# An expert stage in two passes: all first products with the selection work spread between them, activations through DRAM, then all second products

## The chip, the cores and the metric

The kernel runs on one core of one Trainium2 chip. The metric is the device time of one launch in microseconds. Three runs are shown as the time before, and one further execution was profiled.

## The reference

A decoder trunk of two layers on 256 tokens of width 1024. Each layer has a mixer (a linear recurrence beside sparse attention; the change does not touch it), a layer norm, and then the expert stage below, followed by a second layer norm. Inputs, weights and result are float32.

```python
def _peer(x, wq, subkeys, u_tab, v_tab):          # T=256, D=1024, 8 heads, 128 keys, top 16
    q = (xf @ wq).reshape(T, PEER_HEADS, 2, PEER_KEY_DIM)
    s = jnp.einsum('thcd,ckd->thck', q, subkeys)
    sv, si = lax.top_k(s, PEER_TOPK)
    cand = (sv[:, :, 0, :, None] + sv[:, :, 1, None, :]).reshape(T, PEER_HEADS, PEER_TOPK * PEER_TOPK)
    cv, ci = lax.top_k(cand, PEER_TOPK)
    ea = jnp.take_along_axis(si[:, :, 0], ci // PEER_TOPK, axis=-1)
    eb = jnp.take_along_axis(si[:, :, 1], ci % PEER_TOPK, axis=-1)
    experts = (ea * PEER_KEYS + eb).reshape(T, PEER_HEADS * PEER_TOPK)      # of 16384
    gate = jax.nn.softmax(cv, axis=-1).reshape(T, PEER_HEADS * PEER_TOPK)
    act = jax.nn.gelu(jnp.einsum('cd,ced->ce', xf, u_tab[experts]))
    return jnp.einsum('ce,ced->cd', act * gate, v_tab[experts])
```

## The kernel before

The kernel computes the expert stage densely: for all 16384 experts, not only the chosen ones. The experts lie in 128 tiles of 128. For tile `a`, the first product (`u_tile`) multiplies the 512 KB table tile `u_tab[a]` with the transposed tokens and gives 128 experts x 256 tokens; two tiles share a PSUM bank, and after the odd one a gelu writes both, a pair, into a buffer `act` (256 KB). A matrix `G` (two halves of 64 tiles, in SBUF) holds the gate of every expert and token, zero for those not chosen. `w_pair` multiplies a pair by its part of `G`. The second product (`v_tile`) multiplies the result with the 512 KB tile `v_tab[a]` and adds it up in four PSUM banks over all 128 tiles.

Most products are made in three: an operand is split into a high part (`hi`, ScalarE, L104) and the remainder (`lo`, VectorE, or GpSimd for the first 14 tiles, L105), and hi x hi, lo x hi and hi x lo are added up (`col_mm`, L113; `v_mm`, L972). `w_split` (L963, L964) splits an activation in the same way. `raw_mm` (L140) is one plain float32 product that needs no split; it is used for the first products of tiles 14 to 33.

`G` needs the selection first: scores per head (`query`, `top`), two rounds of the best 16 on VectorE (`best16`, `pairs`), the index work of `L847` to `L888`, a transpose of the chosen indices and gates to `eT` and `gT`, and then 32 times `onehots`: two VectorE instructions build one-hot matrices for 8 tokens, TensorE multiplies them, ScalarE copies the product into `G`.

The order before: queries and top-k with 14 first products behind them; index work with first products of tiles 14 to 21; one-hots with those of tiles 22 to 33. Until `G` is there an activation pair can't be used, so these 17 pairs go to DRAM (`kept`, issued by ScalarE, L755). Then the dense loop runs over a sequence `seq` in which the 17 kept pairs are mixed with the 47 fresh ones: it fetches kept pairs (`fetch`, L954) two places ahead, makes first products of fresh pairs two places ahead, and makes the second products of the pair in turn. The last 8 tiles of layer 0 and 6 of layer 1 (`NTBS`) are left for the end, where they are mixed with the layer norm. During the last 16 turns the free parts of `G` take the layer norm's rows, the next layer's first weights and some last `v_tab` tiles (`pre`).

The buffers that set how far one engine may run ahead: `raw` 4 (table tiles as loaded), `hi` and `lo` 3 each, the split activations 4, `act` 8 pairs. A buffer is used again when all readers of its old content are done, and the buffers of one name are given out in the order of the program.

The order of instructions on each engine is fixed when the program is built, by a planner: it takes, in the order of the program, what is ready by its own estimates of durations. On the chip each engine then works through its list in that order.

Of the kernel before, what the change touches and what calls it, by code (L numbers as in the profile page):

```python
# [11 lines left out]
F32 = mybir.dt.float32  # L12
# [36 lines left out]
NACT = 8  # L49
NU0 = 11  # L50
NSP = 17
# [27 lines left out]
def trunk_kernel(ctx: ExitStack, tc: tile.TileContext, x, xt, cst, lam, pvec, brow, w_in, w_lx, w_v, w_q4, lru_w,  # L79
# [187 lines left out]
    for l in range(NL):  # L267
# [12 lines left out]

# [449 lines left out]
        with tc.tile_pool(name="peer", bufs=1, reuse_waits="tile") as pp:  # L730
# [5 lines left out]

# [22 lines left out]
            def u_pair(a0):  # L759
                u_tile(a0)  # L760
                u_tile(a0 + 1)

            with tc.tile_pool(name="topk", bufs=1, reuse_waits="tile") as tk:
                skt = tk.tile([128, 2, 128], F32, name="skt")
                nc.sync.dma_start(skt, sk[l])
                sv = tk.tile([128, 2, 8, 2, 16], F32, name="sv")
# [3 lines left out]
                cd = tk.tile([128, 2, 8, NCAND], F32, name="cd")  # L770
                c2 = tk.tile([128, 2, 8, NCAND], F32, name="c2")
                qhs = {}

                def query(h):
# [4 lines left out]
                    else:  # L779
                        ps = bank()  # L780
                        for c in range(2):
# [3 lines left out]
                            else:  # L785
                                col_mm(ps[:, c * 256:c * 256 + 256], wtile(wq[l, k], (8, 128), POOL), xT)
# [10 lines left out]
                def top(h):  # L797
                    qh = qhs.pop(h)
# [8 lines left out]
                    for tb in range(2):  # L807
                        for c in range(2):
                            k = tb * 2 + c
                            best16(sv[:, tb, h, c], si[:, tb, h, c], ss[:, k], s2[:, k])  # L810

                def pairs(h0, h1):

                    n = h1 - h0
                    a, b, o = sv[:, :, h0:h1, 0], sv[:, :, h0:h1, 1], cd[:, :, h0:h1]
                    for i in range(8):
                        DVE.tensor_tensor(o[:, :, :, OFF[i]:OFF[i] + CNT[i]],
                                          a[:, :, :, i:i + 1].to_broadcast([128, 2, n, CNT[i]]),
                                          b[:, :, :, :CNT[i]], op=ALU.add)
                    DVE.tensor_tensor(o[:, :, :, OFF[8]:NCAND], a[:, :, :, 8:16],  # L820
                                      b[:, :, :, 0:1].to_broadcast([128, 2, n, 8]), op=ALU.add)
                    for h in range(h0, h1):
                        for tb in range(2):
                            best16(cv[:, tb, h], ci[:, tb, h], cd[:, tb, h], c2[:, tb, h])

                query(2)
                q_rows(1)
                query(0)
                top(2)
                query(1)  # L830
                top(0)
                query(3)
                top(1)
                for h in range(4, 8):
                    query(h)
                    top(h - 1)
                    if h == 5:
                        pairs(0, 4)
                top(7)
                for a in range(NPOOL):  # L840
                    u_tile(a)
                pairs(4, 8)

                gt = tk.tile([128, 16, 16], F32, name="gt")
# [428 lines left out]
```

## Time and profile before

| | us |
|---|---|
| three runs: median (lowest, highest) | 1966.04 (1962.35, 1966.09) |
| the profiled execution, its own time | 1961.14 |
| span of its trace | 1959.4 |
| TensorE busy in the span | 1913.2 |
| VectorE, ScalarE, GpSimd busy | 1285.2, 920.1, 126.0 |

The span goes from the first to the last instruction. Busy time counts an engine's instructions; TensorE's matmuls overlap and their ends are modelled, so two starts tell more than one duration. SPq and ACTq are DMA issues of SyncE and ScalarE; a row's time there is that of the issue and not of the transfer. In square brackets stands the idle time before an instruction, and what ended it.

### The profile page before, as it was taken

The numbers are of one execution on the slowest core, as the hardware profiler recorded it, in microseconds if no ns is written. First come the engines' busy times: TensorE is split into PE (matmuls) and PEld (weight loads), VectorE is DVE, ScalarE is ACT, GpSimd is POOL, SyncE is SP. The second block draws the span as 40 slices with busy tenths as digits, with TensorE's granted clock in tenths as the row PEclk, the third lists the DMA queues.
The fourth block names the chain that finished last, engine by engine and source line by source line (L and its number), as shares of the span: only waits on it lengthen the run. The fifth ranks groups of instructions, "written<-read, shape, count | busy, mean of one in ns | idle before, by whom it ended". The sixth has DMA issues, their size and how long they took to land.

```text
span 1959.4 us, 31424 instructions
## 1 busy us (share of the span) xinstructions
PE 1913.2 (98%) x12260; PEld 1676.5 (86%) x12260; DVE 1285.2 (66%) x2477; ACT 920.1 (47%) x1533; POOL 126.0 (6%) x71
## 2 busy tenths in 40 slices
PE   8999899999999999999999998999999999999998
PEld 7758898888888899999877488889888888999997
DVE  5756989565656555565567579896655665556555
ACT  3634425545454444454445344255545445445442
POOL 0005600000000000000000056000000000000000
PEclk9999899999999999999999999999999999999999
DMA  7405453666666666676362055436666676656552
GB/s 279 158 1 157 155 152 110 207 208 197 205 200 220 213 208 210 211 250 191 97 225 66 1 165 159 153 109 220 197 200 200 209 219 213 198 184 221 186 187 93
DMA packets 103017, 344.55 MB, mean 176 GB/s; under 512 B 12626, under 2 KB 13396, under 8 KB 102740
## 3 DMA queue, kind: packets, MB, share of 16 engines
q1 hardware_dynamic: 97972, 333.63, 53.6%
q10 hardware_dynamic: 4896, 8.92, 1.2%
q8 instruction: 96, 1.57, 0.3%
q14 instruction: 53, 0.43, 0.1%
HBM read 332.54 MB, written 9.96 MB: 175 GB/s over the span
## 4 chain that ended last, share of the span: by engine, by line
PE 87%; DVE 8%; DMA 2%; issue 2%; ACT 1%; POOL 1%; SPq 0%; DVEq 0%; POOLq 0%; ACTq 0%
PE ps L972 36%; PE ps L113 34%; PE ps L140 5%; PE ps L120 3%; PE ps L592 3%; DVE og L927 2%; DVE oh L923 2%; PE ps L934 2%; PE ps L564 1%; PE ps L517 1%; DMA raw<-in_wq_dram 1%; DVE si L795 1%; PE ps L233 1%; DVE s L793 1%; POOL lo L105 1%
## 5 line engine op out<-in xcount | busy, mean ns | idle before, releaser
L105 DVE TENSOR_TENSOR lo<-raw,hi 128x1024 fp32r<-128x1024 f32 x460 | 562.6, 1224 | 426.7 <-ACT hi L104 426.6
L104 ACT CAST hi<-raw 128x1024 fp32r<-128x1024 f32 x508 | 532.5, 1050 | 551.3 <-PE ps L113 321.0
L113 PE MATMUL ps<-xThi,hi 128*128 128x256 f32 x2080 | 594.2, 286 | 10.5 <-ACT hi L104 10.5
L113 PE MATMUL ps<-xThi,lo 128*128 128x256 f32 x2080 | 591.3, 284 | 5.9 <-POOL lo L105 5.1
L113 PE MATMUL ps<-xTlo,hi 128*128 128x256 f32 x2080 | 590.8, 284 | 0.0
L972 PE MATMUL ps<-hi,W 128*128 128x512 f32 x1936 | 550.5, 391 | 1.6 <-ACT W L963 1.6
L113 PEld LDWEIGHTS ps<-xThi,hi 128*128 128x128 f32 x2080 | 401.1, 193 | 18.8 <-ACT hi L104 10.9
L972 PEld LDWEIGHTS ps<-hi,W 128*128 128x128 f32 x1936 | 351.9, 189 | 65.8 <-ACT W L963 1.8
L113 PEld LDWEIGHTS ps<-xTlo,hi 128*128 128x128 f32 x2080 | 401.0, 193 | 7.3
L113 PEld LDWEIGHTS ps<-xThi,lo 128*128 128x128 f32 x2080 | 400.7, 193 | 6.6 <-POOL lo L105 5.7
L972 PE MATMUL ps<-lo,W 128*128 128x512 f32 x968 | 299.4, 390 | 0.0
L972 PEld LDWEIGHTS ps<-lo,W 128*128 128x128 f32 x968 | 181.8, 188 | 39.8
L963 ACT CAST W<-act 128x256 fp32r<-128x256 f32 x242 | 92.3, 405 | 145.9 <-PE ps L972 139.0
L140 PE MATMUL ps<-xTf,raw 128*128 128x256 f32 x704 | 158.1, 381 | 0.0
L140 PEld LDWEIGHTS ps<-xTf,raw 128*128 128x128 f32 x704 | 131.5, 190 | 17.6 <-issue 1.0
L105 POOL TENSOR_TENSOR lo<-raw,hi 128x1024 fp32r<-128x1024 f32 x48 | 122.5, 2566 | 329.6 <-ACT hi L104 329.5
L964 DVE TENSOR_TENSOR W<-act,W 128x256 fp32r<-128x256 f32 x242 | 97.3, 421 | 34.0 <-PE ps L972 31.5
L752 ACT ACTIVATE act<-ps 128x512 f32<-128x512 f32 x128 | 76.0, 593 | 92.8 <-PE ps L140 78.6
L950 DVE TENSOR_TENSOR act<-act,G 128x512 f32<-128x512 f32 x128 | 87.8, 686 | 44.5 <-DMA act<-kept 44.5
L938 ACT ACTIVATE G<-ps 128x256 f32<-128x256 f32 x256 | 74.8, 425 | 33.6 <-PE ps L934 31.9
L927 DVE TENSOR_TENSOR og<-oh,gT 128x2048 f16<-128x2048 f16 x64 | 76.0, 1219 | 0.7
L923 DVE TENSOR_TENSOR oh<-iota,eT 128x2048 f16<-128x2048 f16 x64 | 76.1, 1217 | 0.0
(256 smaller groups left out, 1293.0 us busy)
## 6 DMA issues: line engine op xcount, KB each, us to landing
raw<-in_u_tab_dram SPq DMA_DIRECT2D x256, 512.0 KB, 3.6
raw<-in_v_tab_dram SPq DMA_DIRECT2D x256, 512.0 KB, 3.6
raw<-in_w_in_dram SPq DMA_DIRECT2D x24, 512.0 KB, 4.5
raw<-in_wq_dram SPq DMA_DIRECT2D x24, 512.0 KB, 3.9
kept<-act ACTq DMA_DIRECT2D x34, 256.0 KB, 4.0
act<-kept SPq DMA_DIRECT2D x34, 256.0 KB, 4.3
ow<-in_w_out_dram SPq DMA_DIRECT2D x16, 512.0 KB, 7.4
qf<-in_w_q_dram SPq DMA_DIRECT2D x8, 512.0 KB, 3.8
```

Of the source, the lines that this page charges most:

```text
L104: ACT.copy(hi, raw)
L105: lo_eng.tensor_tensor(lo, raw, hi, op=ALU.subtract)
L113: PE.matmul(ps, a[m], b[n], start=start and i == 0, stop=stop and i == 2)
L140: PE.matmul(ps, raw[:, c], xTf[:, c], start=c == 0, stop=c == NCH - 1)
L752: ACT.activation(at.rearrange("p a b -> p (a b)"), ps, AF.Gelu_apprx_tanh)
L923: DVE.tensor_tensor(oh.rearrange("p q w a i -> p (q w) a i"), iota.unsqueeze(1).to_broadcast([128, 8, 128, 2]), eT[:, qs].rearrange("p q w ...
L927: DVE.tensor_tensor(og, oh[:, :, 0:1].to_broadcast([128, 4, 2, 128, 2]), gT[:, qs].unsqueeze(3).to_broadcast([128, 4, 2, 128, 2]), op=ALU. ...
L938: ACT.activation(G[g][:, :, t1:t1 + 4], ps.rearrange("p (t g a) -> p g a t", g=2, a=64)[:, g], AF.Copy, scale=1.0 / GSC)
L950: DVE.tensor_tensor(act[a0], act[a0], G[a0 // 64][:, a0 % 64:a0 % 64 + 2, :], op=ALU.mult)
L963: ACT.copy(whi, at[:, a % 2])
L964: DVE.tensor_tensor(wlo, at[:, a % 2], whi, op=ALU.subtract)
L972: PE.matmul(accs[tb * 2 + hf], ww[m][:, TB[tb]], v[n][:, hf * 512:hf * 512 + 512], start=a == first[0] and (m, n) == (0, 0), stop=a == 127 ...
```

## The change

All 128 first products come first. They are all split products (no `raw_mm` among them), and every activation pair goes to DRAM. The selection work is written as a generator that yields a cost after each piece; between pieces first products are issued so that the sum of costs is balanced, and it works in two halves of four heads. The queries of heads 4 to 7 are split on VectorE. The first products that are left are spread evenly between the 32 one-hot groups, which have buffers of their own. Then a second loop fetches pairs in order, two and three places ahead, and makes all second products. `act` has 4 buffers. Cut to its core:

```diff
-NACT = 8
-NU0 = 11
-NSP = 17
+NACT = 4
             def u_tile(a):
-                if NPOOL <= a < 2 * NSP:
-                    raw_mm(ps[:, HALF[a % 2]], rtile(u_tab[l, a], (8, 128)))
-                else:
-                    col_mm(ps[:, HALF[a % 2]], wtile(u_tab[l, a], (8, 128), POOL if a < NPOOL else DVE), xT)
+                col_mm(ps[:, HALF[a % 2]], wtile(u_tab[l, a], (8, 128), POOL if a < NPOOL else DVE), xT)
                 if a % 2:
                     at = act_tile()
                     ACT.activation(at.rearrange("p a b -> p (a b)"), ps, AF.Gelu_apprx_tanh)
-                    if a // 2 < NSP:
-                        kept[a - 1] = spill.tile([128, 2, S], F32, name="kept%d" % (a - 1), bufs=1)
-                        ACT.dma_start(kept[a - 1], at)
-                    else:
-                        act[a - 1] = at
+                    kept[a - 1] = spill.tile([128, 2, S], F32, name="kept%d" % (a - 1), bufs=1)
+                    ACT.dma_start(kept[a - 1], at)
...
-                                col_mm(ps[:, c * 256:c * 256 + 256], wtile(wq[l, k], (8, 128), POOL), xT)
+                                col_mm(ps[:, c * 256:c * 256 + 256], wtile(wq[l, k], (8, 128), POOL if h < 4 else DVE), xT)
...
+                def choices(g):
+                    DVE.tensor_tensor(gt, cv[:, g], cv[:, g, :, 0:1].to_broadcast([128, 8, 16]), op=ALU.subtract)
+                    ACT.activation(gt, gt, AF.Exp)
...
+                    yield 1.2
...
+                def work():
+                    for h in (2, 0, 1, 3):
+                        yield from top(h)
+                    yield from pairs(0)
+                    yield from choices(0)
+                    for h in range(4, 8):
+                        query(h)
+                        yield 2.44 - 5.76
+                        yield from top(h)
+                    yield from pairs(1)
+                    yield from choices(1)
+                    yield 0.0
+                    yield from turn_round()
...
+                for cost in work():
+                    room -= cost
+                    while room < 0 and a < 96:
+                        u_tile(a)
+                        room += 2.88 if a < NPOOL else 1.66
+                        a += 1
...
-                    oh = ring.tile([128, 4, 2, 128, 2], F16, tag="lo", name="oh")
-                    og = ring.tile([128, 4, 2, 128, 2], F16, tag="hi", name="og")
+                    ohg = (state.tile([128, 2, 4, 2, 128, 2], F16, tag="xTf", name="ohg") if t0 % 16 else
+                           pp.tile([128, 2, 4, 2, 128, 2], F16, name="ohg"))
+                    oh, og = ohg[:, 0], ohg[:, 1]
...
+                a0 = a
                 for i in range(32):
                     onehots(8 * i)
-                    while au < 2 * NSP and (au - 2 * NU0 + 1) * 32 <= (i + 1) * (2 * NSP - 2 * NU0):
-                        u_tile(au)
-                        au += 1
+                    while a < 128 and (a - a0) * 32 < (i + 1) * (128 - a0):
+                        u_tile(a)
+                        a += 1
...
+                seq = list(range(0, 128, 2))
...
                 for j, p in enumerate(body):
                     ready(j + 2)
-                    n = min(more_u(j + 2), len(todo)) if j < len(body) - 1 else len(todo)
-                    for _ in range(max(0, (n + 1) // 2)):
-                        u_tile(todo.pop(0))
+                    ready(j + 3)
                     v_tile(p)
-                    for _ in range(max(0, n - (n + 1) // 2)):
-                        u_tile(todo.pop(0))
                     w_pair(seq[j + 1])
                     v_tile(p + 1)
```

## Rows read from the trace of the kernel before

**Rows 1.** The page, parts 1 and 2: busy time of the engines, and the granted TensorE clock in 40 equal slices (tenths of full speed, 9 is 90% or more).

```profile
PE 1913.2 (98%) x12260; PEld 1676.5 (86%) x12260; DVE 1285.2 (66%) x2477; ACT 920.1 (47%) x1533; POOL 126.0 (6%) x71
PEclk9999899999999999999999999999999999999999
```

**Rows 2.** Busy time by stage: the stretch, its length, then PE, PEld, DVE, ACT and POOL busy (instructions), granted clock, DMA share, GB/s. The first three rows are layer 0 (top-k and index work; one-hots; dense loop), the last two the first two of these stages in layer 1.

```profile
150.00:272.00 122.00, 112.61 (x792) 106.05 (x791) 101.95 (x451) 43.25 (x58) 61.24 (x24) 0.96 0.52 163
272.00:352.00 80.00, 78.80 (x738) 71.27 (x737) 76.91 (x70) 43.39 (x138) 0.00 (x0) 1.00 0.41 122
352.00:935.00 583.00, 581.44 (x3570) 523.81 (x3569) 345.39 (x405) 288.22 (x379) 0.00 (x0) 1.00 0.66 210
...
1130.00:1250.00 120.00, 110.15 (x787) 104.75 (x787) 101.95 (x450) 43.17 (x57) 61.25 (x24) 0.97 0.53 166
1250.00:1326.00 76.00, 74.80 (x718) 67.73 (x717) 74.85 (x67) 40.29 (x132) 0.00 (x0) 1.00 0.40 116
```

**Rows 3.** The same columns in stretches of 10 us, two in the top-k stage of each layer.

```profile
220.00:230.00 10.00, 2.34 (x10) 1.90 (x9) 9.93 (x40) 5.11 (x6) 4.72 (x2) 0.66 0.13 35
230.00:240.00 10.00, 10.00 (x73) 10.00 (x72) 10.00 (x4) 3.29 (x4) 10.00 (x4) 0.83 0.60 194
1190.00:1200.00 10.00, 7.53 (x63) 7.33 (x62) 10.00 (x75) 1.97 (x3) 2.40 (x1) 1.00 0.55 163
1200.00:1210.00 10.00, 4.51 (x21) 4.22 (x22) 9.93 (x16) 5.11 (x6) 7.05 (x3) 0.66 0.26 78
```

**Rows 4.** The waits between 150 and 352 us: who waited for whom, us in total, times, the longest.

```profile
ACT gt L848 <- DVE gt L847: 9.2, 1, 9.2
...
PE ps L113 <- ACT hi L104: 5.1, 1, 5.1
...
PE ps L113 <- POOL lo L105: 2.5, 1, 2.5
```

**Rows 5.** Timeline of TensorE in the one-hot stage: start, time, engine, line, operation, count. One plain float32 first product is 16 entries, one one-hot group 16.

```profile
299.86 3.67 PE L140 MATMUL ps<-xTf,raw 128*128 128x256 f32 x16
303.36 2.00 PE L934 MATMUL ps<-og,oh 128*128 128x128 f16 x32
```

**Rows 6.** Timeline of TensorE in the dense loop: the first matmul of a first product and of the second product behind it; and the first of three second products in a row and of the first product behind them.

```profile
705.60 0.28 PE L113 MATMUL ps<-xThi,hi 128*128 128x256 f32 x1
...
708.48 0.63 PE L972 MATMUL ps<-hi,W 128*128 128x512 f32 x2
...
401.90 0.63 PE L972 MATMUL ps<-hi,W 128*128 128x512 f32 x2
...
410.08 0.28 PE L113 MATMUL ps<-xThi,hi 128*128 128x256 f32 x1
```

**Rows 7.** The page, part 5: groups of instructions, with busy time, mean ns of one, and the idle time before them.

```profile
L105 DVE TENSOR_TENSOR lo<-raw,hi 128x1024 fp32r<-128x1024 f32 x460 | 562.6, 1224 | 426.7 <-ACT hi L104 426.6
...
L964 DVE TENSOR_TENSOR W<-act,W 128x256 fp32r<-128x256 f32 x242 | 97.3, 421 | 34.0 <-PE ps L972 31.5
...
L950 DVE TENSOR_TENSOR act<-act,G 128x512 f32<-128x512 f32 x128 | 87.8, 686 | 44.5 <-DMA act<-kept 44.5
```

**Rows 8.** Timeline of VectorE in the dense loop of layer 0, in a stretch without products with G.

```profile
379.71 0.43 DVE L964 TENSOR_TENSOR W<-act,W 128x256 fp32r<-128x256 f32 x1 [0.48 <-PE ps L972]
380.73 1.23 DVE L105 TENSOR_TENSOR lo<-raw,hi 128x1024 fp32r<-128x1024 f32 x1 [0.59 <-ACT hi L104]
382.43 0.43 DVE L964 TENSOR_TENSOR W<-act,W 128x256 fp32r<-128x256 f32 x1 [0.48 <-PE ps L972]
```

**Rows 9.** Timeline of all engines around one fetch of layer 0, of which SyncE's, VectorE's and one of ScalarE's rows are shown. The first product with G is that of a fresh pair, the second that of the fetched one.

```profile
435.30 0.43 SPq L954 DMA_DIRECT2D act<-kept  x1
...
437.56 0.69 DVE L950 TENSOR_TENSOR act<-act,G 128x512 f32<-128x512 f32 x1
...
438.20 1.05 ACT L104 CAST hi<-raw 128x1024 fp32r<-128x1024 f32 x1 [1.32 <-PE ps L972]
...
439.05 0.69 DVE L950 TENSOR_TENSOR act<-act,G 128x512 f32<-128x512 f32 x1 [0.81 <-DMA act<-kept]
...
439.66 1.22 DVE L105 TENSOR_TENSOR lo<-raw,hi 128x1024 fp32r<-128x1024 f32 x1
...
440.80 0.42 DVE L964 TENSOR_TENSOR W<-act,W 128x256 fp32r<-128x256 f32 x1
```

**Rows 10.** The same around one fetch of layer 1.

```profile
1455.26 0.43 SPq L954 DMA_DIRECT2D act<-kept  x1
...
1460.96 0.69 DVE L950 TENSOR_TENSOR act<-act,G 128x512 f32<-128x512 f32 x1 [2.75 <-DMA act<-kept]
```

**Rows 11.** Timelines of SyncE and ScalarE at the start of the dense loop: two loads for second products, the gelu of the last kept pair, and the fetches of the first two pairs.

```profile
347.18 1.34 SPq L102 DMA_DIRECT2D raw<-in_v_tab_dram  x2
...
352.53 0.60 ACT L752 ACTIVATE act<-ps 128x512 f32<-128x512 f32 x1 [0.69 <-PE ps L140]
...
352.56 0.90 SPq L954 DMA_DIRECT2D act<-kept  x2
```

**Rows 12.** The page, part 6: the fetches (count, KB each, median us from issue to landing); and the view of tile `kept`, which takes writes and fetches together: who waited for it (us, times), and the times to landing.

```profile
act<-kept SPq DMA_DIRECT2D x34, 256.0 KB, 4.3
...
  DVE act L950: 44.5, 30
...
DMA to landing us min/median/max: 2.0/4.1/6.6
```

More of the change, by code (lines that the diff above doesn't have):

```diff
@@ L826, in trunk_kernel @@
[L826 to L844, printed above, removed]
@@ new lines, in top, with pairs @@
+                            best16(sv[:, h // 4, j, c], si[:, h // 4, j, c], ss[:, k], s2[:, k])
+                            yield 1.45
+                def pairs(g):
+                    a, b = sv[:, g, :, 0], sv[:, g, :, 1]
+                    for i in range(8):
+                        DVE.tensor_tensor(cd[:, :, OFF[i]:OFF[i] + CNT[i]], a[:, :, i:i + 1].to_broadcast([128, 8, CNT[i]]),
+                                          b[:, :, :CNT[i]], op=ALU.add)
+                        if i % 4 == 3:
+                            yield 1.2
+                    DVE.tensor_tensor(cd[:, :, OFF[8]:NCAND], a[:, :, 8:16],
+                                      b[:, :, 0:1].to_broadcast([128, 8, 8]), op=ALU.add)
+                    for j in range(8):
+                        best16(cv[:, g, j], ci[:, g, j], cd[:, j], c2[:, j])
+                        yield 1.05
@@ L903, in trunk_kernel @@
-                for a0 in range(2 * NU0 - 2, 2 * NU0, 2):
-                    u_pair(a0)
+                    yield 2.3
+                    DVE.tensor_tensor(t3, t3, sif[:, :, 1].unsqueeze(2).to_broadcast(shp), op=ALU.mult)
+                    yield 1.2
+                    tree(of(ev[:, 1], g), t3)
+                    DVE.tensor_reduce(gs, gt, axis=AX.X, op=ALU.add)
+                    DVE.reciprocal(gs, gs)
+                    DVE.tensor_tensor(of(gate, g), gt.rearrange("p (b h) k -> p b h k", b=2),
+                                      gs.rearrange("p (b h) -> p b h", b=2).unsqueeze(3).to_broadcast([128, 2, 4, 16]), op=ALU.mult)
@@ L906, in trunk_kernel @@
+                for h in (2, 0, 1, 3):
+                    if h == 0:
+                        q_rows(1)
+                    query(h)
+                a, room = 0, 0.0
+                for cost in work():
[4 more added lines that the diff above has]
+                        a += 1
             with tc.tile_pool(name="dense", bufs=1, reuse_waits="tile") as dp:
@@ L985, in v_tile @@
                         v_mm(a, ww, v, tb)
-                seq, k = [], 0
-                for i, f in enumerate(fresh):
-                    while k < NSP and k < 1 + (i + 1) * NSP / (0.55 * len(fresh)):
-                        seq.append(2 * k)
-                        k += 1
-                    seq.append(f)
+                seq = list(range(0, 128, 2))
                 tailp = list(range(nv, 128, 2))
@@ L1042, in trunk_kernel @@
                       [(pre_wv, i) for i in range(3) if more]
[L1043 to L1049 removed]
                 def ready(j):
[L1052 removed]
+                    if j < len(seq) and seq[j] not in act:
                         fetch(seq[j])
@@ L1056, in trunk_kernel @@
                     ready(j)
-                for _ in range(2):
-                    u_tile(todo.pop(0))
                 w_pair(body[0])
@@ L1081, in trunk_kernel @@
                             f(i)
-                assert not pre and not todo, (pre, todo)
+                assert not pre, pre
                 gb = ln_gb(new_gb, (l, 2))
+                for j in range(len(body), len(seq)):
+                    ready(j)
                 for p in tailp[1:]:
```

119 lines of the change are left out of this document (49 added, 70 removed).

## The prediction

> **What bounds the kernel now.** I read the page's shares first: TensorE is busy 98% of the span, VectorE 66%, ScalarE 47% [rows 1]. Busy matmul time overstates, so I read the stages next. From 352 to 935 us (interleaved first and second products of layer 0) TensorE does not pause: 581.4 of 583 us, while VectorE has work for 345 of them, and the DMA engines move 210 GB/s [rows 2]. TensorE sets the pace there and can be made faster only by less work. It loses time only before that: 9.4 us of idling in 150 to 272 us and 1.2 us in 272 to 352, and 9.9 and 1.2 us in the same stages of layer 1 [rows 2]. Within them stand the largest gap and a half clock: in 220 to 230 us TensorE worked 2.34 of 10 us at a granted clock of 0.66, and was at 0.83 in the ten after; in layer 1 4.51 us at 0.66 [rows 3]. The waits say why: ScalarE's exponential of the gates stood 9.2 us for VectorE, with the splits of the next table tiles queued behind it, and TensorE then waited 5.1 us for ScalarE and 2.5 us for GpSimd [rows 4].
>
> **First pass: what the change takes away.** (1) Of each layer's 34 spilled tiles 20 went through the plain float32 product. One takes 3.50 us (from 299.86 to 303.36, [rows 5]); the split product takes 2.88 us (705.60 to 708.48, [rows 6]). 40 tiles at 0.62 us: -25 us.
> (2) TensorE's idling in these stages sums to 21.7 us over both layers [rows 2], and the half clock costs another 4: 10 us at 0.83 lose 1.7, and 2.34 and 4.51 us at 0.66 lose 0.8 and 1.5 [rows 3]. So 26 us are to be had if top-k work is always covered by first products. VectorE can carry it on average: today's 102 us of top-k stage, 77 us of one-hots [rows 2] and 122 low parts (114 table tiles, 8 query tiles) at 1.22 us [rows 7] are 328 us, against 128 x 2.88 + 32 x 0.93 (half of 1.86 us for two one-hot groups, [rows 5]) + 8 x 2.88 = 421 us of TensorE. But in the top-k stretch itself the two are level by the diff's own costs, and the exponential that blocked ScalarE now comes twice per layer. Bounds: all of the 26 us, or none and as much lost again. I take half, -13 us. First pass: -38 us (from -51 to +1).
> (3) The 47 further spills per layer are issued from ScalarE at about 0.4 us each (a fetch's issue takes 0.43, [rows 9]), some 20 us; ScalarE is idle for half of the dense loop [rows 2] and nothing on the path waits for it, so nothing is added. Were ScalarE full it would be these 20 us per layer.
>
> **Second pass: what the change adds.** A second product takes TensorE 2.73 us (three from 401.90 to 410.08, [rows 6]), a pair 5.46. Per pair VectorE has two low parts (1.22), two split remainders (0.42) and one product with G (0.69), 3.97 us [rows 7]. Capacity is there. DMA would be 1.25 MB per pair at 5.46 us, 240 GB/s, beside 210 now [rows 2]; near, but not over.
>
> The price is in a ring. Only four activation buffers are left, and every pair is fetched. The fetch of pair j+3 needs the buffer of pair j-1, free when VectorE has made the remainder of that pair's second tile. Whatever pair number the loop fetches ahead, the ring closes after four. What matters is where the planner puts the product of the fetched pair in VectorE's order. It runs instructions as soon as it believes their inputs are there, not in program order: the first two fetches stand after two loads of second-product tiles that the program issues later, at the moment when the gelu before them in the ring got its buffer [rows 11]. And it believes that a fetch lands sooner than it does: the fetch at 435.30 has its product as the next thing on VectorE at 438.24, but the data let it start at 439.05; in layer 1 it is 1455.26 and 1460.96, a stall of 2.75 us [rows 9, 10]. 30 of 34 fetched pairs stalled VectorE, 44.5 us in all [rows 12]. Today that is hidden: eight buffers, no fetch waits for a recent VectorE instruction, and TensorE runs on from tiles split ahead.
>
> In a steady run of second products VectorE goes remainder 379.71, low part 380.73, remainder 382.43, and so on every 2.72 us, with gaps of about 0.5 us between [rows 8]. Put the changed kernel on this pattern: the remainder ending at 380.14 frees the buffer, the fetch goes at once, and a product put 2.94 us later falls at 383.1, into the gap ahead of the next low part and ahead of the remainder that frees the next buffer (about 385.15). As VectorE works in order, this gives a closed chain: remainder, fetch, landing, product, low part, remainder. Its length: 0.05 (semaphore) + 4.3 from issue to landing [rows 12] + 0.61 from product to low part + 1.14 from low part to remainder [rows 9] + 0.42 [rows 7] = 6.52 us per pair, against TensorE's 5.46. The loss is 1.06 us for each of 60 and 61 pairs in the two layers, 128 us; tiles split ahead cover about 4 us per layer, so +120 us. Bounds: with the quick landing (435.30 to 439.05, 3.75 us, [rows 9]) the chain is 5.97 us and the loss 54 us; with the slow one (5.70 us, [rows 10]) 7.92 us and 290 us. I take the median of the 34 fetches, since each pair adds its own latency and the load is about today's (1.25 MB in 6.5 us is 200 GB/s).
>
> By the Trainium skill, "DMA: Bandwidth & Descriptors", section "Anatomy of one DMA", a transfer costs about 2.0 us and its bytes at 436 GB/s, an estimate of 2.6 us for 256 KB. By that the chain would be 4.8 us and would not bind; the fetches of this trace, at a median of 4.3 us, do not agree.
>
> (4) At the end of the second pass the next layer's weights, last tiles and the layer norm's rows are loaded beside pairs that now take half the time of today's mixed ones; the eight extra high and low parts on VectorE and 16 norm instructions at about 0.7 us go into its waits in part. I add 4 us, from 0 to 10.
>
> **Sum.** -38 + 120 + 4 = +86 us. The profiled execution took 1961.1 us (its span 1959.4), so 2047 us. The median of the three runs shown, 1966.0, is 4.9 us above that execution; a measurement of this kernel tells about 0.2%, or 4 us, from no change.
>
> **Rivals.**
> A: the ring does not bind, since the product is put behind the freeing remainder. Place: VectorE's order, once per pair; it decides when the planner's latency is above some 5.0 us (385.15 less 380.14), or above 3.3 us with a low part in front, which shortens the chain to 5.4 us. For it: in today's rows I know only that the product came before the next low part, 4.0 us after the fetch at most [rows 9]. Against: it stands there each time the data are late. Then the second pass runs at TensorE's pace: -38 + 4, 1927 us (1910 to 1965). This is the case on the other side.
> B: landing is under 3.2 us, so that the chain is below 5.46 us. The quickest of all spill transfers took 2.0 us, the median 4.1 [rows 12], and 30 of 34 were late. Also 1927 us. It is what the rule of the page would give.
> C: the ring is slack and the first pass is worse: the exponential holds ScalarE twice per layer, nothing is recovered and as much is added, -25 + 26 + 5, 1967 us, no change. For it the 9.2 us [rows 4]; against it, tiles split ahead on VectorE and shorter halves.
> D: the product is put ahead of a whole remainder and two low parts: 4.3 + 0.05 + 0.61 + 0.33 + 1.14 + 1.14 + 0.42 = 7.99 us per pair, 2.53 x 121 = 306 us, less 8 and 34, 2225 us. Only if the planner's latency is much under 2 us.
> A half clock in the second pass I leave out: gaps of 2.5 us in ten (1190 to 1200) left it at 1.00 [rows 3].
>
> **Chances.** The forecast 0.60, A 0.23, B 0.05, C 0.07, D 0.05. The forecast's own range, from its bounds: quick landings and the whole first-pass gain, 54 - 51 + 0, give 1964; the median landing with a first pass at +1 and 10 at the end gives 2092; a little slower landings 2100. To hold eight in ten the range reaches into A and B: 1923 to 2100, which leaves out D, the upper end of the forecast and half of A's lower part. Slower: the forecast nearly whole, and D, 0.65. Faster: A and B nearly whole, 0.28. Same: C and the edges, 0.07.
>
> **What would show it.** Right: in the second pass VectorE idles about 3 us per pair before the product with G, released by the fetch; pairs come every 6 to 7 us; TensorE has gaps of about 1 us per pair, and SyncE's fetches follow VectorE's remainder. First pass: no plain float32 product, 2.88 us per tile, less than 13 us of gaps. Wrong: pairs every 5.46 us with TensorE solid (A, B), or gaps of TensorE in the first pass that exceed today's (C). What would upset the sum most is the planner's order on VectorE, which today's trace shows only for rings of eight.

## The result, and the profile after

| | before | after |
|---|---|---|
| median of four runs (lowest, highest), us | 1965.12 (1962.35, 1966.09) | 1986.91 (1984.31, 1991.17) |
| span of the profiled execution | 1959.4 | 1984.6 |
| first load of the selection, layer 0 and layer 1 | 148.9, 1126.1 | 151.1, 1146.7 |

The ratio is 1.0115 (95% interval 1.0094 to 1.0136): 22 us slower, where +82 us over the median had been forecast. By the loads in the last line, layer 0 takes 18.4 us longer, layer 1 4.6 us, and 2.2 us lie ahead of both.

Busy time by stage after, layer 0 (columns as in [rows 2]: stretch, length, PE, PEld, DVE, ACT, POOL, clock, DMA share, GB/s): top-k and index work, one-hots, the rest of the first pass, the boundary between the passes, and the second pass.

```profile
150.00:272.00 122.00, 114.29 (x871) 108.86 (x869) 81.53 (x315) 54.96 (x72) 39.24 (x16) 0.97 0.58 186
272.00:352.00 80.00, 74.00 (x595) 72.88 (x594) 66.44 (x196) 35.65 (x45) 0.00 (x0) 0.96 0.60 193
352.00:620.00 268.00, 268.00 (x2479) 266.67 (x2479) 169.68 (x141) 142.84 (x248) 0.00 (x0) 1.00 0.63 202
620.00:640.00 20.00, 15.12 (x61) 12.32 (x60) 12.45 (x19) 8.12 (x14) 0.00 (x0) 0.83 0.64 210
640.00:780.00 140.00, 140.00 (x620) 115.91 (x619) 95.86 (x129) 75.30 (x103) 0.00 (x0) 1.00 0.74 241
...
780.00:860.00 80.00, 73.39 (x310) 58.32 (x309) 52.14 (x73) 37.33 (x52) 0.00 (x0) 0.98 0.76 244
860.00:940.00 80.00, 76.91 (x328) 60.44 (x327) 51.88 (x69) 42.15 (x59) 0.00 (x0) 1.00 0.83 272
```

Two things are to be seen. The second pass is not slow from its start: 640 to 780 us has no gap. It loses time at its end, and more than the busy column says: at full pace 80 us hold 354 second-product matmuls (a row of the kernel with halved fetches, below), here they hold 310 and 328. That is 70 fewer at 80/354 = 0.226 us, some 16 us. And the first pass, which was to lose its gaps, has them at three places in each layer. Here they are in layer 0 in stretches of 5 us, with the waits that stand in them:

```profile
210.00:215.00 5.00, 1.73 (x13) 1.34 (x11) 4.93 (x32) 1.82 (x3) 0.50 (x1) 0.97 0.00 0
215.00:220.00 5.00, 2.25 (x11) 2.14 (x11) 5.00 (x5) 3.18 (x4) 2.80 (x1) 0.50 0.35 101
...
340.00:345.00 5.00, 1.06 (x10) 0.82 (x8) 4.97 (x6) 1.54 (x2) 0.00 (x0) 0.94 0.62 175
345.00:350.00 5.00, 4.85 (x31) 4.86 (x32) 3.67 (x4) 1.32 (x4) 0.00 (x0) 0.50 0.25 91
...
620.00:625.00 5.00, 1.16 (x10) 0.96 (x8) 1.87 (x3) 1.54 (x2) 0.00 (x0) 0.93 0.66 211
625.00:630.00 5.00, 3.95 (x9) 3.15 (x10) 3.19 (x7) 1.42 (x4) 0.00 (x0) 0.50 0.86 309
```

```profile
ACT gt L834 <- DVE gt L833: 7.4, 1, 7.4
...
PE ps L111 <- ACT hi L102: 3.3, 1, 3.3
...
PE ps L111 <- POOL lo L103: 2.7, 1, 2.7
...
PE ps L945 <- DVE ohg L938: 4.1, 1, 4.1
...
PE ps L983 <- ACT W L974: 4.9, 1, 4.9
```

The first place is the exponential's, as in [rows 4], with two waits of TensorE behind it (3.3 and 2.7 us). The second is new: TensorE has run all first products issued so far and waits for the first one-hots. The third, also new, is the boundary: the first fetches are issued behind table loads, and the second products wait for the first split activation. After each, TensorE ran at a granted clock of 0.50, the 1.2 GHz level, in the next five microseconds. The kernel before had one such place in layer 0, and by stretches of five microseconds its clock falls as low: TensorE was busy for 0.14 us of 220 to 225 us, and at 0.50 in 225 to 230 (the 0.66 of [rows 3] is a mean over ten).

The chain in the second pass, in VectorE's timeline and in SyncE's (fetches only), first in the stretch without gaps. A remainder (L975) is the rest of a split activation, a low part (L103) that of a table tile, and the landing is the time from a fetch's issue until VectorE has the data:

```profile
663.07 0.42 DVE L975 TENSOR_TENSOR W<-act,W 128x256 fp32r<-128x256 f32 x1
...
667.38 0.69 DVE L961 TENSOR_TENSOR act<-act,G 128x512 f32<-128x512 f32 x1 [0.97 <-DMA act<-kept]
667.99 0.42 DVE L975 TENSOR_TENSOR W<-act,W 128x256 fp32r<-128x256 f32 x1
...
672.41 0.69 DVE L961 TENSOR_TENSOR act<-act,G 128x512 f32<-128x512 f32 x1 [2.38 <-DMA act<-kept]
673.02 1.22 DVE L103 TENSOR_TENSOR lo<-raw,hi 128x1024 fp32r<-128x1024 f32 x1
674.16 0.42 DVE L975 TENSOR_TENSOR W<-act,W 128x256 fp32r<-128x256 f32 x1
```

```profile
663.56 0.42 SPq L965 DMA_DIRECT2D act<-kept  x1
...
668.44 0.33 SPq L965 DMA_DIRECT2D act<-kept  x1
...
674.65 0.42 SPq L965 DMA_DIRECT2D act<-kept  x1
```

Remainder, fetch, landing, product, remainder: the closed chain is there. But a low part stands between product and remainder only in every second pair (in 12 of 25 products of 645 to 780 us). In the two steps shown a fetch follows the one before it after 4.88 and 6.21 us; over the 25 products the mean distance is 5.46 us, TensorE's own pace. So here the chain costs nothing.

It does so at the end of layer 0's second pass. From 780 to 940 us a low part stands between in 18 of 26 pairs, nine times in a row around these lines (again VectorE, then the fetch between them on SyncE):

```profile
842.10 0.69 DVE L961 TENSOR_TENSOR act<-act,G 128x512 f32<-128x512 f32 x1 [1.87 <-DMA act<-kept]
842.71 1.22 DVE L103 TENSOR_TENSOR lo<-raw,hi 128x1024 fp32r<-128x1024 f32 x1
843.84 0.42 DVE L975 TENSOR_TENSOR W<-act,W 128x256 fp32r<-128x256 f32 x1
...
850.44 0.69 DVE L961 TENSOR_TENSOR act<-act,G 128x512 f32<-128x512 f32 x1 [4.71 <-DMA act<-kept]
```

```profile
844.33 0.42 SPq L965 DMA_DIRECT2D act<-kept  x1
```

The landings are longer there too (median 4.1 us and up to 6.0 in 780 to 860 us, against 3.8 and 4.4 before 780), and products come 6.23 us apart. The chain as it was forecast, with a landing of 4.1, gives 6.3. For 25 distances 0.77 us over TensorE's pace are 19 us, and tiles split ahead cover about 4: that is the 16 us counted above. In layer 1 (1780 to 1900 us) it is 10 of 21 pairs and 5.74 us, and less is lost.

The page sums VectorE's waits for the fetches, and shows the landing over the whole pass; against [rows 7, 12] four times the waiting at a shorter landing:

```profile
L961 DVE TENSOR_TENSOR act<-act,G 128x512 f32<-128x512 f32 x128 | 88.4, 692 | 172.9 <-DMA act<-kept 170.3
...
kept<-act ACTq DMA_DIRECT2D x128, 256.0 KB, 2.5
act<-kept SPq DMA_DIRECT2D x128, 256.0 KB, 3.8
```

### The profile page after: what moved, and what is told of

It is laid out like the page before. It is cut to its first block, busy times and chain, and to the rows that moved or that the text cites. A ratio compares the mean times of both kernels' runs of the same rounds, so it can differ in the third digit from the quotient of the medians.

```text
span 1984.6 us, 32589 instructions
## 1 busy us (share of the span) xinstructions
PE 1910.3 (96%) x12580; PEld 1681.0 (85%) x12580; DVE 1322.8 (67%) x2553; ACT 976.4 (49%) x1579; POOL 82.0 (4%) x55
## 4 chain that ended last, share of the span: by engine, by line
PE 80%; DMA 9%; DVE 6%; issue 2%; ACT 1%; POOL 0%; SPq 0%; POOLq 0%; DVEq 0%; ACTq 0%
PE ps L111 41%; PE ps L983 25%; DMA act<-kept 6%; PE ps L945 3%; PE ps L589 3%; PE ps L118 2%; DVE lo L103 2%; DMA raw<-in_v_tab_dram 1%; PE ps L231 1%; PE ps L797 1%; PE ps L561 1%; PE ps L514 1%; DVE W L975 1%; PE ps L369 0%; POOL lo L103 0%
## 5 line engine op out<-in xcount | busy, mean ns | idle before, releaser
L103 DVE TENSOR_TENSOR lo<-raw,hi 128x1024 fp32r<-128x1024 f32 x516 | 629.6, 1222 | 267.3 <-ACT hi L102 266.8
L111 PE MATMUL ps<-xThi,hi 128*128 128x256 f32 x2400 | 692.0, 288 | 6.5 <-ACT hi L102 6.5
L111 PE MATMUL ps<-xThi,lo 128*128 128x256 f32 x2400 | 683.5, 285 | 8.3 <-POOL lo L103 6.0
L111 PE MATMUL ps<-xTlo,hi 128*128 128x256 f32 x2400 | 682.8, 285 | 0.0
L111 PEld LDWEIGHTS ps<-xThi,lo 128*128 128x128 f32 x2400 | 463.6, 193 | 10.6 <-POOL lo L103 6.9
L111 PEld LDWEIGHTS ps<-xThi,hi 128*128 128x128 f32 x2400 | 464.1, 193 | 7.9 <-ACT hi L102 6.9
L111 PEld LDWEIGHTS ps<-xTlo,hi 128*128 128x128 f32 x2400 | 464.1, 193 | 0.3
L975 DVE TENSOR_TENSOR W<-act,W 128x256 fp32r<-128x256 f32 x242 | 101.0, 420 | 10.3 <-PE ps L983 8.1
L103 POOL TENSOR_TENSOR lo<-raw,hi 128x1024 fp32r<-128x1024 f32 x32 | 78.5, 2460 | 315.5 <-ACT hi L102 315.5
L938 DVE TENSOR_TENSOR ohg<-ohg,gT 128x2048 f16<-128x2048 f16 x64 | 78.2, 1225 | 2.1
L945 PE MATMUL ps<-ohg 128*128 128x128 f16 x1024 | 71.5, 222 | 8.2 <-DVE ohg L938 8.2
L934 DVE TENSOR_TENSOR ohg<-iota,eT 128x2048 f16<-128x2048 f16 x64 | 77.9, 1220 | 1.7 <-PE ps L945 1.7
```

Source lines behind the costliest of these rows:

```text
L103: lo_eng.tensor_tensor(lo, raw, hi, op=ALU.subtract)
L111: PE.matmul(ps, a[m], b[n], start=start and i == 0, stop=stop and i == 2)
L934: DVE.tensor_tensor(oh.rearrange("p q w a i -> p (q w) a i"), iota.unsqueeze(1).to_broadcast([128, 8, 128, 2]), eT[:, qs].rearrange("p q w ...
L938: DVE.tensor_tensor(og, oh[:, :, 0:1].to_broadcast([128, 4, 2, 128, 2]), gT[:, qs].unsqueeze(3).to_broadcast([128, 4, 2, 128, 2]), op=ALU. ...
L945: PE.matmul(ps[:, k * 128:k * 128 + 128], oh[:, q, 1, :, i], og[:, q, w, :, i], start=w == 0, stop=w == 1)
L975: DVE.tensor_tensor(wlo, at[:, a % 2], whi, op=ALU.subtract)
```

## Experiments on the first pass

All times are medians of at least four runs; the kernel before had 1964.0 to 1965.0 us beside them. Edits are to the changed kernel (1986.9 us).

**Plain products back for 20 tiles.**

```diff
+                if NPOOL <= a < 34:
+                    raw_mm(ps[:, HALF[a % 2]], rtile(u_tab[l, a], (8, 128)))
+                else:
                     col_mm(...)
```

> The first products of tiles 14 to 33 go through the plain float32 product again, as before the change, and so need no low part on VectorE. If TensorE sets the pace of the first pass, 40 tiles at 0.62 us add 25 us: 2012 us. Rival, VectorE's low parts are what makes the gaps of the top-k stretch (6 us and a half clock at 205 to 225, 4 us at 341): part of them goes, and the time is 1985 to 2000 us.

2005.7 us, ratio 1.0211 (1.0194 to 1.0228): +19 of the 25. The shorter products are a real gain of the change, most of it on the path.

**The exponentials late.** Both softmaxes move behind the index work.

```diff
                     yield from choices(1)
+                    softmax(0)
+                    softmax(1)
```

> The softmax of the first four heads' gates is made together with that of the last four, at the end of the selection work. Theory: the gap of TensorE at 210 to 217 us and its half clock after it (some 8 us per layer) come from ScalarE's exponential that stands 7.4 us for VectorE with two splits behind it; without it the time is 1971 to 1977 us. Rival: VectorE is late as such, and its low parts or another ScalarE instruction make the same gap: 1983 to 1990 us.

1991.9 us, 1.0145 (1.0127 to 1.0162): a miss, nothing gained. TensorE still waits there, 4.0 us in place of 6.0, mostly for GpSimd's low part (200 to 240 us):

```profile
PE ps L111 <- POOL lo L103: 2.9, 1, 2.9
PE ps L111 <- ACT hi L102: 1.1, 1, 1.1
```

**No exponential.** This kernel leaves out `ACT.activation(gt, gt, AF.Exp)`.

> Leaves out the exponential of the gates (they stay differences of scores, so the weights are not those of the reference). Theory: ScalarE's 7.4 us wait for VectorE ahead of the exponential delays the high parts behind it, from which TensorE's gap of 6.0 us and the half clock after it come in each layer: about 8 us per layer, -16 us, 1971 us. Rival: VectorE is the late one in that stretch and the low parts come too late whatever ScalarE does: within 5 us of the changed kernel.

1988.2 us, 1.0122 (1.0105 to 1.0138): the time is the rival's. With the exponential gone one wait of TensorE is left in 205 to 232 us, for VectorE, where there were two:

```profile
PE ps L111 <- DVE lo L103: 3.3, 1, 3.3
```

So ScalarE's 7.4 us explain less than half of the waiting there (2.7 of 6.0 us). TensorE got 2.7 us back in 200 to 240 us (36.65 us at 0.96, against 33.98 at 0.91), but the whole kernel did not get faster, and where the gain went is not shown. What is late besides is VectorE, full in that stretch (9.93 of 10 us in 210 to 220 us of the changed kernel).

**The last three pairs kept.** First products in the order 6 to 127, 0 to 5; the last three pairs stay in their buffers and are used first, so that the second pass starts without a fetch.

```diff
+                a = (n + 6) % 128
...
+                    if a < 6:
+                        act[a - 1] = at
+                        return
```

> First products are made in the order of tiles 6 to 127, 0 to 5, and the last three pairs made are not sent to DRAM but used first in the second pass. Theory: the gap of 4.9 us between the passes and the half clock after it (some 7 us per layer) come from the first fetch, which SyncE could issue only at 620.9 us; now only the last one-hot group is waited for: -8 to -14 us, 1973 to 1979 us. Rival: the gap is moved to the first fetched pair: 1984 to 1990 us.

1961.9 us, 0.9984 (0.9972 to 0.9996): -25, twice what was expected. The boundary of layer 0 (600 to 640 us) went from 35.12 us at 0.91 to full speed, which is 4.9 us of gap and 0.09 x 40 = 3.6 us of clock. In layer 1 it was 34.85 us at 0.96, 5.2 and 1.6 us: 15 us for both, where the expectation had some 7 for each and took from half to all of it. Another 5 us came from the end of layer 0's second pass, and some 4 from its 200 to 240 us (36.06 us at 0.96, against 33.98 at 0.91); neither had been expected.

```profile
600.00:640.00 40.00, 40.00 (x264) 36.08 (x263) 25.05 (x33) 22.19 (x38) 0.00 (x0) 1.00 0.61 204
780.00:985.00 205.00, 199.55 (x859) 158.65 (x859) 140.38 (x206) 102.21 (x151) 0.00 (x0) 1.00 0.71 238
```

**Cover for the one-hots**, on top of that: `yield 0.0` ahead of the last step of the selection becomes `yield 5.8`, so that two more first products are issued before the first one-hots.

> The last three pairs kept and two more first products issued before the one-hots, without the spread loads. The cover took 7 us off the kernel with both others; the spread loads cost 6 us beside the kept pairs. If the parts add up: 1962 - 7 = 1955 us. If each only shifts the planner's order in stages it does not touch, anything from 1955 to 1967 us.

1955.5 us, 0.9946 (0.9929 to 0.9962): -6.4, and faster than the kernel before. In the last pairs' kernel 335 to 370 us had TensorE busy for 30.92 us at 0.90; now

```profile
200.00:240.00 40.00, 33.85 (x265) 33.45 (x263) 38.29 (x112) 16.53 (x20) 8.44 (x4) 0.91 0.54 171
335.00:370.00 35.00, 33.51 (x297) 33.26 (x296) 23.93 (x23) 16.66 (x25) 0.00 (x0) 1.00 0.62 205
```

2.6 us of gap and 0.10 x 35 = 3.5 us of clock are gone in layer 0, and the wait for the first one-hots fell from 4.1 to 1.5 us in both layers. But the stretch of 200 to 240 us, which the edit does not touch, gave some 4 us back.

## Experiments on the second pass

**Five buffers** (`NACT = 5`), and **the product on GpSimd** (`POOL.tensor_tensor` for `DVE.tensor_tensor` in `w_pair`).

> The changed kernel (1986.9 us) with five activation buffers in place of four. Theory of the chain: the planner puts the product with G right where it believes the fetch has landed, ahead of the remainder that frees the next buffer, whatever the number of buffers; so the chain stays, VectorE still stands some 170 us for fetches, and the time is 1981 to 1990 us. Rival, the ring is too short: one more pair ahead covers the landing, the second-pass gaps of some 22 us go, and the time is about 1965 us.

> The product with G is made on GpSimd in place of VectorE, nothing else. Theory of the chain: GpSimd stands for the fetches instead, VectorE makes remainders and low parts without waiting for them, TensorE has no gaps after 640 us (17.5 us in layer 0, 5 us in layer 1 now), and the time is about 1965 us (1960 to 1970). Rival, the loads of second-product tiles are late because of DMA load: the same waits of TensorE for low parts stay, 1983 to 1990 us.

1987.5 us, 1.0113 (1.0096 to 1.0130), and 2017.6 us, 1.0271 (1.0254 to 1.0288). The fifth buffer changes nothing: VectorE still waits 182.6 us for fetches, and in 780 to 940 us products come 6.18 us apart, at 13 low parts in 26 pairs and a longer landing (median 5.7 us in the second half of the stretch; its profiled execution took 1995.6 us). The second is a miss, and it does not show whether the chain was broken: 640 to 780 us has no gap, but it had none before. A product takes twice as long on GpSimd, and the loads into parts of `G` that it frees held SyncE, and with it the table loads (in 640 to 960 us SyncE stood 98.8 us for products ahead of such loads, 31.3 in the changed kernel):

```profile
L961 POOL TENSOR_TENSOR act<-act,G 128x512 f32<-128x512 f32 x128 | 181.8, 1423 | 1330.8 <-DMA act<-kept 1284.6
```

**The loads into freed G**: spread over every second turn from the 27th turn before the end (for every turn from the 14th), or put on GpSimd's queue, or that with the product on GpSimd too.

```diff
-                    if left <= 14 and pre:
+                    if left <= 27 and left % 2 and pre:
```

> The loads for the next layer and the last tiles are issued in every second turn from the 27th before the end, not in every turn from the 14th. Theory: in most of the second pass the chain (5.5 us a pair) just keeps up with TensorE, and it binds from 780 us on because these loads lengthen the landing of the fetches; half the load per turn takes some 10 of the 17.5 us of layer 0, and the time is about 1977 us. Rival, the late gaps are due to the order on VectorE alone: no change, 1984 to 1990 us.

> The changed kernel (1986.9 us); the loads into freed parts of G (layer norm rows, next layer's weights) are issued from GpSimd's queue in place of SyncE's, at the same places of the program. Theory, SyncE is held: SyncE stands 31 us in layer 0 for products with G before these loads, and the loads of second-product tiles and the fetches stand behind them; with that gone the gaps from 780 us on go, -10 to -18 us, 1969 to 1977 us. Rival, DMA load: the same bytes move at the same time, so no change, 1984 to 1990 us.

> Both the product with G and the loads into freed parts of G are on GpSimd. If the 31 us that the product on GpSimd alone cost are the loads of second-product tiles that stood on SyncE behind loads into G, which waited for late products, this takes them and the chain's gaps away: 1960 to 1970 us. Rival, GpSimd's products hold VectorE up or come too late by themselves: 2000 us or more.

1976.1 us, 1.0055 (1.0036 to 1.0074): -11 as expected. 1994.8 us, 1.0154 (1.0130 to 1.0178): +8, a miss. 2003.4 us, 1.0209 (1.0188 to 1.0231): better by 14 than the product alone on GpSimd, but in the range of the rival. And with the last pairs kept, the spread loads no longer gain:

> The last three pairs kept and the loads spread, together. The one alone took 25 us off the changed kernel, the other 11. If the first works at the pass boundary (gap of 4.9 us and 3.6 us lost to the half clock per layer, 17 us) and the second at the end of the second pass, they add up: 1987 - 36 = 1951 us. If the shifted order of the first already took away the late gaps of the second pass (it has 5.5 us left in 780 to 985 us, the changed kernel 10.5), only its remainder of some 3 us is left to gain: 1959 us.

1967.6 us, 1.0021 (1.0011 to 1.0031), 6 us more than without the spreading; with the cover besides (expected -12 to -14 against that) 1960.8 us, 0.9975 (0.9964 to 0.9986). So the loads bear on the late gaps, but are not their whole cause. What they do seems to hang on VectorE's order, which each edit shifts: with the loads spread, a low part stands in the chain in 11 of 28 pairs of 780 to 940 us, not in 18 of 26.

**Half a fetch.** Only the first of the two tiles of a pair is fetched; the second is set to zero, so this kernel leaves out half of the products.

```diff
-                    nc.sync.dma_start(act[a0], kept[a0])
+                    nc.sync.dma_start(act[a0][:, 0], kept[a0][:, 0])
+                    POOL.memset(act[a0][:, 1], 0.0)
```

> Leaves out half of each fetched activation tile (the second table row of each pair is set to zero by GpSimd, so that these products are zero): 128 KB per fetch in place of 256, 16 MB less in all. Theory: the chain remainder, fetch, landing, product, remainder is at TensorE's pace (5.55 us against 5.46 a pair) and goes over it where transfers slow down; with a quicker landing (3.8 us to some 3.2) it falls to about 5 us a pair and the late gaps of the second pass go: -15 to -22 us, 1965 to 1972 us, and VectorE waits under 120 us for fetches in place of 170. Rival: the late gaps come from loads into freed G that hold SyncE until VectorE's products; then the quicker landing changes little, 0 to -6 us.

1982.2 us, 1.0085 (1.0066 to 1.0103): -5. The test did not change what it was to change: the landing fell from 3.8 to 3.6 us only, and a low part still stands in the chain in 16 of 27 pairs of 780 to 940 us. By the Trainium skill, "DMA: Bandwidth & Descriptors", section "Anatomy of one DMA", 128 KB less at 436 GB/s are an estimate of 0.3 us, and 2.0 us do not go with the bytes; the section tells this of transfers issued from GpSimd, and these fetches go out from SyncE. The 0.2 us measured agree with that estimate, and the 3.4 us or so that are left are more than the 2.0 us.

```profile
act<-kept SPq DMA_DIRECT2D x128, 128.0 KB, 3.6
```

**The product done twice.** 0.69 us more in the chain.

> The product with G is done twice for each fetched pair (so the weights hold G squared): 0.69 us more on VectorE per pair, 4.66 of TensorE's 5.46 us. Theory: VectorE, the fetch and the landing form a closed chain of about 5.55 us a pair that holds the product in it; it becomes 6.24 us, and 121 pairs lose 0.7 us each: +85 us, 2070 us, with gaps of TensorE from the first pairs of the second pass on. Rival: the chain is slack by more than that (the planner shifts the product, or a pair more of lead exists), and VectorE has the capacity: 0 to +10 us.

1984.7 us, 1.0105 (1.0088 to 1.0121): no change, a miss for the chain as I had it. VectorE's order says why: in every second pair the second product now stands behind the remainder, where it is not in the chain. Pairs come 5.5 us apart in 645 to 780 us, at TensorE's pace, as without the edit. So the length of the chain is not fixed; the planner lays it out anew for each program.

```profile
660.15 0.69 DVE L961 TENSOR_TENSOR act<-act,G 128x512 f32<-128x512 f32 x1 [0.66 <-DMA act<-kept]
660.76 0.42 DVE L976 TENSOR_TENSOR W<-act,W 128x256 fp32r<-128x256 f32 x1
661.10 0.69 DVE L962 TENSOR_TENSOR act<-act,G 128x512 f32<-128x512 f32 x1
```

**Fetches from GpSimd's queue** (`nc.gpsimd.dma_start` in `fetch`).

> The fetches go out from GpSimd's queue, not behind the table loads in SyncE's order; nothing else changes. Halving a fetch shortened its landing by 0.2 us only (3.8 to 3.6 us), so what it waits for is not its own bytes. Theory: part of the landing is the table load ahead of it in the same queue, and SyncE's order holds the fetch; alone it lands in under 3.2 us, the chain is at most 5 us a pair and the late gaps of the second pass go: -12 to -22 us, 1965 to 1975 us. Rival: the 16 DMA engines are shared whatever the queue, and GpSimd's issue is slower: landing of 3.8 us or more, no gain, or up to +50 us where it reaches 4.2 us.

2109.9 us, 1.0738 (1.0684 to 1.0793): +123 us, at a median landing of 3.6 us. Here VectorE's order has a low part between product and remainder in every pair (21 of 21 in 645 to 780 us, 23 of 23 in 780 to 940), and the chain is the one of the prediction; behind its timeline stands the stretch that was gapless in the changed kernel:

```profile
702.82 0.42 DVE L975 TENSOR_TENSOR W<-act,W 128x256 fp32r<-128x256 f32 x1
...
703.64 0.54 POOL L965 DMA_DIRECT2D act<-kept  x1 [5.73 <-DVE W L975]
...
708.03 0.69 DVE L961 TENSOR_TENSOR act<-act,G 128x512 f32<-128x512 f32 x1 [3.32 <-DMA act<-kept]
708.64 1.22 DVE L103 TENSOR_TENSOR lo<-raw,hi 128x1024 fp32r<-128x1024 f32 x1
709.77 0.42 DVE L975 TENSOR_TENSOR W<-act,W 128x256 fp32r<-128x256 f32 x1
```

```profile
640.00:780.00 140.00, 127.56 (x531) 98.84 (x530) 79.69 (x111) 64.92 (x89) 11.76 (x22) 0.99 0.60 207
```

Products come 6.32 us apart in the first stretch, 6.99 in the second. Some 0.3 us of it is GpSimd's later issue (0.82 us from the remainder's start to the fetch, 0.49 on SyncE), 1.13 the low part, and in the second stretch the median landing is 4.2 us. With the last pairs kept and the cover the same edit gave 2081.5 us, 1.0582 (1.0548 to 1.0617): +126 there.

**Each fetch in two halves.** This one takes the low part out of most steps of the chain, with the bytes unchanged.

```diff
-                    nc.sync.dma_start(act[a0], kept[a0])
+                    [nc.sync.dma_start(act[a0][:, i], kept[a0][:, i]) for i in range(2)]
```

> Each fetch goes out as two transfers of 128 KB behind one another, with the same bytes. The planner then takes the fetched pair to land later and sets its product behind the next low part; in the order of VectorE a remainder follows the product at once in nearly every pair, where in the changed kernel a low part stands between in every second pair (and in nearly every pair where the fetches had a queue of their own, which cost 123 us). Theory: this low part in the chain is what decides between 5.0, 5.5 and 6.5 us a pair; without it the chain is 0.49 + 3.8 to 4.1 + 0.61 = 4.9 to 5.2 us, under TensorE's 5.46, and the late gaps of the second pass go: -12 to -22 us, 1965 to 1975 us, also where transfers are slow. Rival: the second half lands 0.4 us or more later behind the first, with as many more issues on SyncE, and the late gaps come from loads that arrive late and not from the order: no change or up to +10 us.

1963.1 us, 0.9994 (0.9985 to 1.0004): -23.8 us. The landing is as before (3.7 us); VectorE waits 83 us for fetches, not 170; TensorE waits 1.5 us for low parts in both second passes, not 13.0; a remainder follows the product directly in 24 of 24 pairs of 645 to 780 us and 23 of 27 of 780 to 930, and the late stretches are full (two rows by stage, then two of VectorE's timeline):

```profile
780.00:860.00 80.00, 80.00 (x354) 66.23 (x353) 60.28 (x83) 42.45 (x58) 0.00 (x0) 1.00 0.87 288
860.00:940.00 80.00, 78.49 (x343) 63.83 (x342) 58.65 (x78) 46.45 (x65) 0.00 (x0) 1.00 0.86 283
```

```profile
669.55 0.68 DVE L961 TENSOR_TENSOR act<-act,G 128x512 f32<-128x512 f32 x1
670.16 0.42 DVE L975 TENSOR_TENSOR W<-act,W 128x256 fp32r<-128x256 f32 x1
```

The selection's load of layer 1 comes at 1128.4 us (1146.7 after) and the span is 1960.4 (1984.6): 18 us from layer 0, 6 from layer 1. DMA moves more in 780 to 940 us than in the changed kernel (288 and 283 GB/s, not 244 and 272), with the same loads beside the fetches, so the amount moved was not the limit. Smaller transfers alone are not what gained: the half fetches above, with a low part in 16 of 27 pairs there, gained 5 us.

**All three**: last pairs kept, cover, and halves.

> The last three pairs kept, two more first products ahead of the one-hots (together 1955.5 us), and the fetches in two halves. If the order without a low part in the chain takes away what is left of the late gaps (about 5 us per layer): 1943 to 1949 us. If the halves only land later: 1955 us or up to 10 us more.

1941.7 us, 0.9889 (0.9873 to 0.9906): -14 more, 23 us faster than the kernel before and 45 faster than the change as made.

## Why the prediction was right and wrong

- **The sign** was right (slower), the size was not: +22 against +82, for two steps that failed in opposite directions. That the sign came out is luck: with the chain at its measured 22 us, my own sum is -38 + 22 + 4 = -12, faster. The spans' +25 us are by stage: -25 from shorter first products, some +24 from gaps and half clock in the first pass, some +22 from the second pass, +2 ahead of both layers.
- **Step (1), -25 us**, held: putting the 20 tiles back costs 19.
- **Step (2), -13 us**, failed in sign, near its upper bound of +26. Idle and lost clock of layer 0's first pass are 7.7 + 6.0 + 4.9 us and 0.03 x 114 + 0.04 x 74 + 0.17 x 15 = 9 us, against 10.6 and, reckoned in the same way, 0.04 x 113 = 4.5 before [rows 2]; in layer 1 it is some 11 us more than before. I took a cover on average for a cover at each moment: 328 us of VectorE fit beside 421 of TensorE, but not at the end of top-k, and not ahead of the first one-hots. The boundary between the passes was not in my sum at all; it costs 8.5 us in layer 0 and 6.8 in layer 1. That the exponential would block twice (rival C) was wrong too: it blocks once per layer, and taking it out halves the wait of TensorE there but gains no time in all.
- **Step (3), spills at nothing**, held: they land in 2.5 us, and TensorE has no gap in 352 to 620 us.
- **The chain, +120 us**, was right as a mechanism and mis-sized, below its lower bound of 54: about 22 us. The term that failed is "0.61 from product to low part + 1.14 from low part to remainder", taken for each of 121 pairs from one row of the kernel before. From 645 to 780 us it holds in every second pair, products come at TensorE's pace (5.46 us), and nothing is lost; only from 780 to 940 us of layer 0 does it hold in most (18 of 26, 6.23 us apart), and there most of the time goes. Where a program has it in nearly every pair (the fetches from GpSimd's queue), it takes 147 us more than the kernel with halved fetches, which has it in few, 1.21 per pair; less the 0.3 of the later issue that is near the 1.06 forecast. The shorter landing (3.8 for 4.3 us) is the smaller part before 780 us; in 780 to 860 us it was 4.1. The 0.05 us from remainder to fetch were 0.07 (663.49 to 663.56). The kernel with five buffers, with 13 low parts in 26 pairs, lost as much there at longer landings, so order and landing seem to count together, and what lengthens the landing is open.
- **The estimate by the Trainium skill** beside the chain and rival B (2.6 us for 256 KB, from "DMA: Bandwidth & Descriptors", section "Anatomy of one DMA") comes from figures that the section gives for transfers issued from GpSimd, and I set it against fetches from SyncE. The runs agree with it on neither queue: the medians were 3.6 us from GpSimd and 3.8 from SyncE.
- **Step (4), 4 us**, can't be told apart: the loads that it prices stand in the stretch where the chain loses its time, and spreading them gained 11 us, but shifted the order as well.
- **Rival A** named the deciding point, the place of the product in VectorE's order, and half of it came true. Its own pass, without the chain's loss, is the kernel with halved fetches: 1963 us, not 1927, as the first pass had lost what A took for gained. **Rival B** fell: no kernel's median landing of a fetch was under 3.4 us. **D** did not occur in the stretches counted.
- **The signs I named**: gaps of TensorE did not appear in each pair of the changed kernel, only at the ends of the second passes (18 waits for low parts, 13.0 us in all); VectorE's idling before the product, up to 2.4 us, did in 645 to 780 us, while TensorE was solid. That idling is no proof of a loss: VectorE waits for the fetch there although TensorE sets the pace, since the planner put the product first.
- **Open**: how much of the exponential's place is VectorE's, why loads on a queue of their own cost 8 us, why the spread loads gain alone and lose beside the kept pairs, and what takes the last microseconds of the second pass (860 to 940 us, 78 of 80).

## What to carry to other kernels

Where a planner fixes an order per engine, a loop through a transfer has no fixed length: price it with and without each instruction that the planner may set into it, and look at that order before trusting either. An edit that shifts this order, and nothing of the bytes (here each fetch in two halves), can be worth more than a buffer or a queue. A stage that is covered on average still has gaps at its seams (the last selection step, the first fetch after a pass); keep the last results of a pass on chip for the first use of the next, and count the clock behind each gap.

## What the runs showed of the hardware

- Gaps of TensorE of 3.3, 4.1 and 4.9 us were each followed by a granted clock of 0.50 in the next five microseconds; the one of 4.9 us at the boundary of layer 0 went with 3.6 us of lost clock, and both were gone with it.
- A fetch of 128 KB landed in 3.6 us, of 256 KB in 3.8, and two of 128 KB behind one another in 3.7 each.
- The product of 128 x 512 float32 took 1423 ns on GpSimd and 692 on VectorE.
